# A two-layer hybrid trunk on one core: an ordered block for the first layer, a moved residual step, a rearranged last head and another form of the final norm

## The chip, the cores and the metric

The kernel runs on one core of one Trainium2 chip. The metric is the device time of one execution in microseconds (us). The engines have their own instruction queues and run beside each other: PE (TensorE, matmuls; PEld is its weight load), DVE (VectorE), ACT (ScalarE), POOL (GpSimd) and SP (SyncE, which here only issues DMAs). An engine takes its instructions strictly in the order in which they stand in its queue; an instruction that waits for a semaphore holds up all that stand behind it.

## The reference: what is computed

128 context tokens and 512 latent tokens (640 together, five tiles of 128) of width 1024 go through two layers. Layer 0 is gated grouped-query attention, 16 heads of 64 on 4 key/value heads; layer 1 is a bidirectional gated linear recurrence with 8 heads of 128.

```
for i in range(DEPTH):                                   # DEPTH = 2
    sh, sc, g = split(silu(cond) @ ada_w[i] + ada_b[i])  # adaLN, for c and for c_ctx
    h = x * (1 + sc) + sh
    if i % 2 == 0: out = attention(h)   # q,k RMS norm, axial rotary, softmax, silu gate, w_out
    else:          out = rec_mix(h)     # two scans, RMS norm of o, silu gate, w_out
    x = layer_norm(ALPHA * x + g * out, ln_gain[i], ln_bias[i])
```

All is float32. The outputs are both token sets after layer 1, the new key/value cache and the new states.

## The kernel before

Each float32 operand of a projection is split into a high and a low part (ACT casts the high part, DVE or POOL subtracts it to get the low one), and each product takes three matmuls: high by high, low by high, high by low. Activations stand with features on the partitions and the 640 tokens along the row, so that most tiles are 128x640. Times below are us from the start of the span.

*Lead-in (0 to 72).* The adaLN weights of layer 0 come in eight chunks of 1 MB, one for each 128 features of the input. For each chunk PE forms the products (`adaps`, L264), DVE and PE turn them into shift and scale (`ada_row`, `ada_out`), the input is modulated and split, and PE adds this slice's share of keys and values (`acc`, `kv_mms`). SP issues the loads of these chunks and of the weights (`raw`, through a ring of buffers) in one queue. Then comes the first q projection (`pmm`).

*Gate and attention (72 to 362).* The silu gate's projections (`gps`, L335 to 337) run beside the norm and rotary of q, which ends in split tiles `qs` that PE transposes (`qps`, L587) and ACT casts to `X`. For each of the four key/value heads come 16 score tiles of 128 queries by 640 keys (64 in all): PE forms `sc` (L730, L731), DVE takes the row maximum (L824), ACT the exponent with its sum (L827), DVE the reciprocal `rc` (L831), POOL multiplies `p` by it (L832), PE transposes `p` (`pt`, L839), the transposes are copied to `pts` (L735), and PE multiplies with the values (`pot`, L757). The q projection of the next head group, adaLN chunks and the split of the output weights are side work: `weave(att, side, SIDE_B)` lets the side generators emit pieces between those of attention by planned costs.

*Out projection and norm of layer 0 (362 to 445).* `out_mms` (L1002 to 1006) and the class `Norm`; its result goes to DRAM (`x1d`) and, transposed, to the input of layer 1.

*Recurrent heads (445 to 840).* Each of the 8 heads has its five projections (`rps`, `vgps`) on PE, and the scan `gla_gen` of the head before stands between them: seven levels in which PE forms 32 to 128 wide blocks (`lv`), DVE multiplies the decays into A (L1276, L1281) and halves their tables. Behind the scan come the states (`kp`, `sp`), the output (`op`), its RMS norm (`rsqrt`, a DVE and a POOL instruction), two DVE products into `on`, the transposes `oT` and the split `ghi`, `glo`. The class `Residual` (L1359 on) works on the side: `Residual.step()` takes up to two pieces of 128x256 of layer 0's result from DRAM, multiplies by the gain and adds the bias on POOL (L1379, L1380), stores them to `x1a`, and issues the next two loads, all on POOL's queue. There are 20 pieces. It is called at scan level 4, behind the copies to `At`, and behind each head's `rsqrt`.

*Last head and final norm (789 to 876).* The last head has no next projection beside it. `tail_gen` fills PE with parts of the output projection of layer 1 over the heads that are done (`out_part(tt, ks)`: token tile `tt`, heads `ks`, six matmuls for each head) and with four gate spreads (`spread`, L307 and L308: four transposes each, and a copy to `gate`). When the last head's `glo` is there, the five token tiles get their last head's share, and `Norm(1, tt, ...)` runs for each: `y` = `outp` times gate (L1026), plus the residual (L1027), `bn_stats` and `bn_aggr` (L1028, L1033), `rsqrt`, then (y − mean) times gain (L1042) and times rstd plus bias (L1043), each in two halves of 512 columns, and the output's DMA in two halves on SP and ACT. The fifth tile, the context's, runs last and in quarters.

What sets the order: the program is emitted by generators, and the framework's scheduler orders each engine's instructions from it by their dependences; those in `tc.keep_in_program_order` keep their place among each other. Before the change no part of the program is set apart from the rest.

Of the kernel before, what the change touches and what calls it, by code (L numbers as in the profile page):

```python
# [11 lines left out]
F32 = mybir.dt.float32  # L12
# [120 lines left out]
def hybrid_step(ctx: ExitStack, tc: tile.TileContext, a: dict, o: dict):  # L133
# [30 lines left out]
            self.st.close()  # L164


    small = const.tile([P, 66], F32, name="small")
    nc.scalar.dma_start(small, a["small"])
    sel = small[:, 16:18]
# [18 lines left out]
    def rsqrt(out, in_, scale, eps):  # L188
        n = in_.shape[-1]
        t = tiny.tile([P, NKV * TT], F32, tag="rs", name="rs_t")  # L190
        nc.vector.tensor_scalar(t[:, :n], in_, scale, eps, ALU.mult, ALU.add)  # L191
        nc.gpsimd.tensor_tensor(out, t[:, :n], mhalf[:, :n], ALU.pow)
# [105 lines left out]
        nc.vector.tensor_tensor(gcol, src, bias, ALU.add)  # L298
        return None if layer else lambda: spread(layer, c4, gcol)

    def spread(layer, c4, gcol):

        ps = bank1("gateps")
        for s in range(2):
            for j in range(2):
                col = bass.AP(gcol.tensor, gcol.offset + 2 * j + s, [list(gcol.ap[0]), [0, P]])
                nc.tensor.matmul(ps[:, (2 * s + j) * P:(2 * s + j + 1) * P], col, ident, start=True, stop=True)  # L307
        nc.vector.tensor_copy(gate[layer][:, :, c4 * CW:(c4 + 1) * CW], ps[:].rearrange("p (a b) -> p a b", a=2))  # L308

    def ada_gen(chunks):  # L310
        todo, last = None, None
# [676 lines left out]
    rings[:] = [wr]  # L988


    ph = Phase(4, 0)
    h1p = rpool("h1p", 1)
    h1lo = h1p.tile([P, KT, NT], F32R, tag="h1lo", name="h1lo")
# [14 lines left out]
    class Norm:  # L1008
        def __init__(self, layer, tt, ps=None, parts=2):
            self.layer, self.tt, self.w = layer, tt, D // parts  # L1010
            if layer == 0:
                ps = bank2("outp")
            self.ps = ps and [ps[:, nh, :] for nh in range(2)]
            if layer == 0:
                self.x = lnp.tile([P, D], F32, tag="x", name="x", bufs=2)
                nc.scalar.dma_start(self.x, xd[tt])
            else:
                self.x = resid.pop(tt)
            self.y = lnp.tile([P, D], F32, tag="y", name="y", bufs=2)
            self.st = tiny.tile([P, parts, 6], F32, tag=f"st{parts}", name="st")  # L1020

        def part(self, n, ps):
            s = slice(n * self.w, (n + 1) * self.w)
            y = self.y[:, s]
            g = gate[self.layer][:, 1 if self.tt == TS else 0, s]
            nc.vector.tensor_tensor(y, ps, g, ALU.mult)  # L1026
            nc.vector.scalar_tensor_tensor(y, self.x[:, s], ALPHA, y, ALU.mult, ALU.add)  # L1027
            nc.vector.bn_stats(self.st[:, n, :], y)  # L1028

        def finish(self):  # L1030
            x, y = self.x, self.y
            mv = tiny.tile([P, 2], F32, tag="mv", name="mv")
            nc.vector.bn_aggr(mv, self.st[:].rearrange("p a b -> p (a b)"))  # L1033
            rt = tiny.tile([P, 8], F32, tag="rstd", name="rstdl")
            rstd = rt[:, 0:1]
            rsqrt(rstd, mv[:, 1:2], 1.0, LN_EPS)
            for nh in range(2):
                s = slice(nh * 512, (nh + 1) * 512)
                if self.layer == 0:
                    nc.vector.tensor_scalar(y[:, s], y[:, s], mv[:, 0:1], rstd, ALU.subtract, ALU.mult)  # L1040
                else:
                    nc.vector.scalar_tensor_tensor(x[:, s], y[:, s], mv[:, 0:1], lng[:, s], ALU.subtract, ALU.mult)  # L1042
                    nc.vector.scalar_tensor_tensor(x[:, s], x[:, s], rstd, lnb[:, s], ALU.mult, ALU.add)  # L1043
                    (nc.sync, nc.scalar)[nh].dma_start(yd[self.tt][:, s], x[:, s])
            if self.layer == 0:
                nc.sync.dma_start(x1d[self.tt], y)

    drain(split_gs(range(6, 8)))
    h1hi = gsp.tile([P, KT, NT], F32R, tag="gs", name="h1hi")
# [178 lines left out]
    def gla_gen(h, H, last=False):  # L1228
# [30 lines left out]
        for lev in range(7):  # L1259
            nb = NT // (2 * w)  # L1260
            pt = wide(bank2("lv"))
            for c in range(TT):
                if lev < 5:
                    for b in range(4):
                        t0 = c * P + 32 * b
                        queue(nc.tensor.matmul(pt[32 * b:32 * b + 32, 32 * c:32 * c + 32], kc[:, t0:t0 + 32],  # L1266
                                               view(A, QB + t0, [[2 * w, 16 // w], [QF - QB + w, 2], [1, w]]),
                                               start=True, stop=True), c + b == 0)
                else:
                    for b in range(P // w):  # L1270
                        ko, qo = (KB, QB) if b % 2 else (KF, QF)
                        s0, t0 = c * P + w * b, c * P + w * (b ^ 1)
                        queue(nc.tensor.matmul(pt[w * b:w * b + w, w * c:w * c + w], A[:, ko + s0:ko + s0 + w],
                                               A[:, qo + t0:qo + t0 + w], start=True, stop=True), c + b == 0)
            kv = view(A, KF, [[KB - KF + w, 2], [2 * w, nb], [1, w]])
            nc.vector.tensor_tensor(kv, kv, view(cur, 1, [[2 * nb - 1, 2], [2, nb], [0, w]]), ALU.mult)  # L1276
            if lev < 4:
                kc = kcopy(2 * w)
            qv = view(A, QB, [[QF - QB + w, 2], [2 * w, nb], [1, w]])
            nc.vector.tensor_tensor(view(nxt, 0, [[1, 2 * nb]]), view(cur, 0, [[2, 2 * nb]]), view(cur, 1, [[2, 2 * nb]]), ALU.mult)  # L1280
            nc.vector.tensor_tensor(qv, qv, view(cur, 2 * nb + 1, [[-2 * nb - 1, 2], [2, nb], [0, w]]), ALU.mult)  # L1281
            if lev == 0:
                nc.scalar.copy(near, pt[:, :32 * TT])
            elif lev < 5:
                merge(lev, pt)
            if lev == 4:
                pt = wide(bank2("dg"))
                for c in range(TT):
                    for b in range(4):
                        t = slice(c * P + b * 32, c * P + (b + 1) * 32)  # L1290
                        nc.tensor.matmul(pt[32 * b:32 * b + 32, 32 * c:32 * c + 32], H["kd"][:, t], H["q"][:, t], start=True, stop=True)
                merge(0, pt)
                for b in range(4):
                    r = slice(32 * b, 32 * b + 32)
                    nc.gpsimd.tensor_copy(blocks(At[r, :], P)[:, :, r], blocks(near[r, :], 32))  # L1295
                residual.step()
            elif lev > 4:
                for b in range(P // w):
                    r, o_ = slice(w * b, w * b + w), slice(w * (b ^ 1), w * (b ^ 1) + w)
                    nc.scalar.copy(blocks(At[r, :], P)[:, :, o_], blocks(pt[r, :w * TT], w))  # L1300
            cur, nxt = nxt, cur
            w *= 2
            yield D_LEV
# [35 lines left out]
            nc.scalar.activation(on[:, cc], opw[:, cc], AF.Square, accum_out=ss[:, c:c + 1])  # L1339
        rstd = tiny.tile([P, 8], F32, tag="rstd", name="rstdo")  # L1340
        rsqrt(rstd[:, :TT], ss[:, :TT], 1.0 / P, NORM_EPS)
        residual.step()
        nc.vector.tensor_tensor(on[:].rearrange("p (a b) -> p a b", a=TT), opw[:, :NT].rearrange("p (a b) -> p a b", a=TT),
                                view(rstd, 0, [[1, TT], [0, P]]), ALU.mult)
# [68 lines left out]
    def out_part(tt, ks):  # L1413
        if tt not in outs:
            outs[tt] = bank2("outp")
        for k in ks:
            for nh in range(2):
                out_mms(outs[tt][:, nh, :], tt, nh, ghi, glo, [k], queued=(k, nh) == (ks[0], 0))

    for h in range(RH):  # L1420
        H = {} if h else H
        for n, dt in enumerate(proj_gen(h, H, False) if h else first):
            lane.advance(dt)
            if h == RH - 1 and n in (12, 14, 20, 21):
                wo_split((12, 14, 20, 21).index(n))
        if h == RH - 1:
            out_part(0, (0, 1))
        lane.add(gla_gen(h, H, h == RH - 1))
    while residual.todo or residual.live:
        residual.step()  # L1430
# [4 lines left out]

    def tail_gen():
        yield
        out_part(1, (0, 1))
        lane.finish(1)
        wo_split(4)  # L1440
        yield
        splits = iter((5, 6, 7))
        for tt, ks in ((0, (2, 3)), (1, (2, 3)), (0, (4, 5)), (1, (4, 5)), (0, (6,)), (1, (6,))):
            out_part(tt, ks)
            for n in splits:
                wo_split(n)
                break
            yield
        gate[1] = g2.tile([P, 2, D], F32, tag="A", name="gate1")
        for i in range(4):  # L1450
            spread(1, i, gcol1[:, i])
            if i % 2:
                yield
        out_part(2, (0, 1, 2))
        yield
        out_part(2, (3, 4, 5, 6))
        yield

    resid = {}
# [115 lines left out]
```

## Time and profile before

| | |
|---|---|
| median of 3 runs | 878.02 us (876.84 to 880.31) |
| profiled execution | 877.56 us |
| its span | 875.8 us, granted TensorE clock 0.992 |
| lead-in and first q projection (0 to 72) | 58.00 + 14.00 us, PE busy 46.49 + 14.00 |
| gate stage (72 to 125) | 53.00 us, PE busy 50.10 |
| out projection, norm 0 (362 to 445) | 83.00 us, PE busy 82.06 |
| seven heads (445 to 789) | 344.00 us, PE busy 340.80 |

The other stages stand with the prediction. A row of the timeline reads: start, duration of one, engine, line, operation, tile written and tiles read with their shapes, how many in a run, and in brackets the idle time of the engine before it and what ended that. A row of the waits reads: the waiting engine and line, what it waited for, total us, times, longest. PE's matmuls overlap: a fill matmul of 0.39 us starts 0.23 us behind the one before.

### The profile page before, as it was taken

To read this page: it belongs to the slowest core of one execution; us is meant where nothing else is said; L and a number is where in the kernel's file an instruction comes from. 1 tells how busy PE (TensorE), PEld (TensorE's weight loads), DVE (VectorE), ACT (ScalarE), POOL (GpSimd) and SP (SyncE) were. 2 spreads that over 40 slices of the span, in tenths; PEclk is the share of its full clock that TensorE was granted. 3 is DMA by queue.
4 is the path that set the end of the run, shared out by engine and by line. 5 is a ranking of instruction groups with operands and counts; after the bars stand their busy time and mean duration, and the time that the engine had idled before them with its cause. 6 is when DMAs were issued, how large, how long until landed. Compare 5 with 4: busy or idle time off the path is not lost. (4 is left out here: it accounts for less than half of the span.)

```text
span 875.8 us, 19258 instructions
## 1 busy us (share of the span) xinstructions
PE 828.6 (95%) x8124; PEld 736.7 (84%) x8124; DVE 533.2 (61%) x966; ACT 369.9 (42%) x732; POOL 205.5 (23%) x247
## 2 busy tenths in 40 slices
PE   6898999989999899899999999999999999999895
PEld 3588999878877666678999999999999999997785
DVE  3457335565746655586637486666667575848468
ACT  2232436544745765612434453444444434444200
POOL 0132002422424643610000132233232212111111
PEclk9999999999999999999999999999999999999998
DMA  9931112212212037171232313222322323212113
GB/s 358 407 113 55 61 61 73 98 49 98 97 49 98 1 124 261 56 280 60 72 97 65 91 55 120 61 98 79 101 83 68 81 90 109 89 47 74 55 52 117
DMA packets 30182, 89.86 MB, mean 103 GB/s; under 512 B 4400, under 2 KB 9008, under 8 KB 29072
## 3 DMA queue, kind: packets, MB, share of 16 engines
q1 hardware_dynamic: 19728, 72.03, 23.2%
q0 software_dynamic: 3168, 9.31, 4.0%
q10 hardware_dynamic: 7200, 7.29, 2.6%
q8 instruction: 64, 1.05, 0.5%
q14 instruction: 22, 0.18, 0.1%
HBM read 79.44 MB, written 9.18 MB: 101 GB/s over the span
## 5 line engine op out<-in xcount | busy, mean ns | idle before, releaser
L1128 PE MATMUL rps<-h1hi,rhi 128*128 128x320 f32 x368 | 117.0, 318 | 0.0
L1129 PE MATMUL rps<-h1lo,rhi 128*128 128x320 f32 x368 | 113.5, 308 | 0.0
L1130 PE MATMUL rps<-h1hi,rlo 128*128 128x320 f32 x368 | 113.4, 308 | 0.0
L832 POOL TENSOR_SCALAR p<-p,rc 128x640 f32<-128x640 f32 x64 | 54.1, 847 | 95.2 <-DVE rc L831 84.0
L224 DVE TENSOR_TENSOR rlo<-raw,rhi 128x1024 fp32r<-128x1024 f32 x32 | 46.1, 1444 | 42.7 <-ACT rhi L223 42.7
L1128 PEld LDWEIGHTS rps<-h1hi,rhi 128*128 128x128 f32 x368 | 69.2, 188 | 1.3
L1130 PEld LDWEIGHTS rps<-h1hi,rlo 128*128 128x128 f32 x368 | 69.1, 188 | 0.2 <-DVE rlo L224 0.2
L1129 PEld LDWEIGHTS rps<-h1lo,rhi 128*128 128x128 f32 x368 | 69.0, 188 | 0.0
L824 DVE TENSOR_REDUCE nm<-sc 128x1 f32<-128x640 f32 x64 | 52.3, 820 | 25.0 <-PE sc L731 24.5
L827 ACT ACTIVATE p<-sc,nm 128x640 f32<-128x640 f32 x64 | 51.1, 799 | 25.7 <-DVE nm L824 18.6
L223 ACT CAST rhi<-raw 128x1024 fp32r<-128x1024 f32 x32 | 33.5, 1050 | 60.4 <-PE rps L1129 56.2
L839 PE MATMUL pt<-ident,p 128*128 128x128 f32 x320 | 50.7, 278 | 5.3 <-POOL p L832 3.1
L1239 ACT COPY kc<-A 128x640 f32<-128x640 f32 x40 | 32.5, 812 | 51.0 <-PE lv L1266 31.8
L1118 PE MATMUL vgps<-rhi,h1hi 128*128 128x256 f32 x180 | 51.1, 284 | 0.0
L1120 PE MATMUL vgps<-rhi,h1lo 128*128 128x256 f32 x180 | 50.7, 282 | 0.0
L1119 PE MATMUL vgps<-rlo,h1hi 128*128 128x256 f32 x180 | 50.4, 280 | 0.0
L735 ACT COPY pts<-pt 128x512 f32<-128x512 f32 x64 | 36.2, 589 | 31.6 <-PE pt L839 31.3
L1295 POOL COPY At<-near 32x160 f32<-32x160 f32 x32 | 10.0, 313 | 165.6 <-DVE near L1256 164.6
L839 PEld LDWEIGHTS pt<-ident,p 128*128 128x128 f32 x320 | 37.3, 142 | 13.5 <-POOL p L832 4.8
L730 PE MATMUL sc<-kk,X 128*128 128x320 f32 x128 | 43.5, 347 | 2.4 <-ACT p L827 2.2
L335 PE MATMUL gps<-hhi,whi 128*128 128x320 f32 x128 | 40.8, 319 | 2.4 <-ACT X L589 2.4
L1118 PE MATMUL vgps<-wspare,h1hi 128*128 128x256 f32 x140 | 41.6, 297 | 0.0
(265 smaller groups left out, 2403.2 us busy)
## 6 DMA issues: line engine op xcount, KB each, us to landing
raw<-in_rec_w_in SPq DMA_DIRECT2D x40, 512.0 KB, 4.3
raw<-in_ada_w SPq DMA_DIRECT2D x32, 512.0 KB, 3.9
raw<-in_ada_w SPq DMA_DIRECT2D x8, 1024.0 KB, 11.2
raw<-in_attn_w_in SPq DMA_DIRECT2D x16, 512.0 KB, 5.0
raw<-in_attn_w_out SPq DMA_DIRECT2D x8, 512.0 KB, 5.4
raw<-in_rec_w_out SPq DMA_DIRECT2D x8, 512.0 KB, 4.2
h<-in_xT SPq DMA_DIRECT2D x8, 320.0 KB, 10.0
x1d<-y SPq DMA_DIRECT2D x5, 512.0 KB, 2.8
```

Source lines behind the costliest of these rows:

```text
L224: pin((lo_eng or nc.gpsimd).tensor_tensor(lo, raw, hi.bitcast(F32), ALU.subtract))
L730: nc.tensor.matmul(out, X[:, h, t0:t0 + P], kk[:, c, k0:k1], start=True, stop=False)
L824: nc.vector.tensor_reduce(nm[:, 0:1], sc[:, :, :320], AX.XY, ALU.max, negate=True)
L827: nc.scalar.activation(halves(p[:]), sc[:, :, :320], AF.Exp, bias=nm[:, 0:1], accum_out=su[:, 0:1])
L832: nc.gpsimd.tensor_scalar(p, p, rs[:, 0:1], 1.0, ALU.mult, ALU.mult)
L839: nc.tensor.transpose(pt[:, i * 256 + q * P:i * 256 + (q + 1) * P], ps[q][:, (k0 + i) * P:(k0 + i + 1) * P], ident)
L1118: nc.tensor.matmul(out, h1hi[:, k, t], hi, start=(k == 0), stop=False)
L1119: nc.tensor.matmul(out, h1hi[:, k, t], lo, start=False, stop=False)
L1120: nc.tensor.matmul(out, h1lo[:, k, t], hi, start=False, stop=(k == KT - 1))
L1128: nc.tensor.matmul(ps[:, j, :320], hi[:, k, :], h1hi[:, k, t], start=(k == 0), stop=False)
L1129: nc.tensor.matmul(ps[:, j, :320], hi[:, k, :], h1lo[:, k, t], start=False, stop=False)
L1130: nc.tensor.matmul(ps[:, j, :320], lo[:, k, :], h1hi[:, k, t], start=False, stop=(k == KT - 1))
```

## The change

Four edits.

1. Everything from the first loads to the end of attention is put into a block of its own, `tc.block(name="lead", schedule_with_timeline_sim=True)`. Within it the scheduler orders by a simulated time line. At its end each engine branches (L993 of the changed kernel) to what follows; there is no barrier there.
2. `residual.step()` is taken from scan level 4 and called twice behind each head's `rsqrt`.
3. `tail_gen` is rearranged: `out_part(1, (0,))` comes ahead of the last head's scan, the spreads go one at a time between the scan's levels with their copies on ACT (`nc.scalar.copy`), and more of the fill stands ahead of `op` and between `op` and `oT`.
4. For the four latent tiles the norm of layer 1 is formed another way (`finish_two_pass`): ACT copies `y` with a running sum, multiplies the sum by −1/D, and squares y − mean with a running sum; DVE makes two products over all 1024 columns; one DMA on SP writes the tile.

```diff
+    blk = tc.block(name="lead", schedule_with_timeline_sim=True)
+    blk.__enter__()
     small = const.tile([P, 66], F32, name="small")
...
-    def spread(layer, c4, gcol):
+    def spread(layer, c4, gcol, eng=None):
...
-        nc.vector.tensor_copy(gate[layer][:, :, c4 * CW:(c4 + 1) * CW], ps[:].rearrange("p (a b) -> p a b", a=2))
+        (eng or nc.vector.tensor_copy)(gate[layer][:, :, c4 * CW:(c4 + 1) * CW], ps[:].rearrange("p (a b) -> p a b", a=2))
...
+    blk.__exit__(None, None, None)
     ph = Phase(4, 0)
...
+            self.two_pass = layer == 1 and tt < TS
...
-            nc.vector.bn_stats(self.st[:, n, :], y)
+            if not self.two_pass:
+                nc.vector.bn_stats(self.st[:, n, :], y)
...
+        def finish_two_pass(self, rstd):
+            x, y = self.x, self.y
+            junk = lnp.tile([P, D], F32, tag="sq", name="sq")
+            sums = tiny.tile([P, 4], F32, tag="mv2", name="mv2")
+            nc.scalar.activation(junk, y, AF.Copy, accum_out=sums[:, 0:1])
+            nc.scalar.mul(sums[:, 1:2], sums[:, 0:1], -1.0 / D)
+            nc.scalar.activation(junk, y, AF.Square, bias=sums[:, 1:2], accum_out=sums[:, 2:3])
+            nc.vector.scalar_tensor_tensor(x, y, sums[:, 1:2], lng, ALU.add, ALU.mult)
+            rsqrt(rstd, sums[:, 2:3], 1.0 / D, LN_EPS)
+            nc.vector.scalar_tensor_tensor(x, x, rstd, lnb, ALU.mult, ALU.add)
+            nc.sync.dma_start(yd[self.tt], x)
...
                     nc.gpsimd.tensor_copy(blocks(At[r, :], P)[:, :, r], blocks(near[r, :], 32))
-                residual.step()
...
         residual.step()
+        residual.step()
...
         if h == RH - 1:
             out_part(0, (0, 1))
+            out_part(1, (0,))
         lane.add(gla_gen(h, H, h == RH - 1))
...
-        out_part(1, (0, 1))
+        out_part(1, (1,))
         lane.finish(1)
+        out_part(0, (2,))
         wo_split(4)
         yield
-        splits = iter((5, 6, 7))
-        for tt, ks in ((0, (2, 3)), (1, (2, 3)), (0, (4, 5)), (1, (4, 5)), (0, (6,)), (1, (6,))):
-            out_part(tt, ks)
-            for n in splits:
-                wo_split(n)
-                break
+        out_part(0, (3,))
+        out_part(1, (2,))
+        wo_split(5)
+        yield
+        gate[1] = g2.tile([P, 2, D], F32, tag="A", name="gate1")
+        for i, (tt, k) in enumerate(((1, 3), (0, 4), (0, 5), (1, 4))):
+            out_part(tt, (k,))
+            spread(1, i, gcol1[:, i], nc.scalar.copy)
+            if i < 2:
+                wo_split(6 + i)
             yield
-        gate[1] = g2.tile([P, 2, D], F32, tag="A", name="gate1")
-        for i in range(4):
-            spread(1, i, gcol1[:, i])
-            if i % 2:
-                yield
-        out_part(2, (0, 1, 2))
+        out_part(1, (5,))
         yield
-        out_part(2, (3, 4, 5, 6))
+        out_part(0, (6,))
+        out_part(1, (6,))
+        yield
+        out_part(2, (0, 1))
+        yield
+        out_part(2, (2, 3, 4, 5))
+        yield
+        out_part(2, (6,))
         yield
```

Where the scheduler puts the rows now is seen best at three places. Each row has its place in the engine's queue, the line (the changed kernel's lines are higher by 2 to 19), the operation, the tile written and those read, the shape and how many in a run.

The first is PE at the end of attention, the last score tiles of the last head group; `X_2730` and `X_2731` are the same q tile. Before:

```order
1444 L731 MATMUL sc<-klo,X_2730 128x320
1445 L839 MATMUL pt<-ident,p 128x128 x6
1446 L730 MATMUL sc<-kk,X_2730 128x320
1447 L731 MATMUL sc<-klo,X_2730 128x320
1448 L730 MATMUL sc<-kk,X_2730 128x320
1449 L731 MATMUL sc<-klo,X_2730 128x320
1450 L839 MATMUL pt<-ident,p 128x128 x3
1451 L730 MATMUL sc<-kk,X_2730 128x320
```

And now:

```order
1443 L733 MATMUL sc<-klo,X_2731 128x320
1444 L841 MATMUL pt<-ident,p 128x128 x10
1445 L732 MATMUL sc<-kk,X_2731 128x320
1446 L733 MATMUL sc<-klo,X_2731 128x320
1447 L732 MATMUL sc<-kk,X_2731 128x320
1448 L733 MATMUL sc<-klo,X_2731 128x320
1449 L759 MATMUL pot<-pts,vv 64x256 x10
1450 L841 MATMUL pt<-ident,p 128x128 x16
```

Two pairs of `sc` rows are one score tile. Before, the transposes come in threes and sixes between the score tiles; now they stand in runs of ten and more, and a product with the values stands between the last score tile and the transposes behind it.

The second is SP in the lead-in: the loads of the input (`h`), of the adaLN chunks (`ada_w`, raw_170 to raw_279 before, raw_171 to raw_280 now, 1 MB each), of the key/value weights and of the q and gate weights (`attn_w_in`, 512 KB each). Before:

```order
15 L200 DMA h_106<-in_xT 128x640
16 L208 DMA raw_198<-in_ada_w 128x2048
17 L200 DMA h_106<-in_xT 128x640
18 L200 DMA ck<-in_cache_k 128x256
19 L208 DMA raw_236<-in_ada_w 128x2048
20 L211 DMA raw<-in_attn_kv 128x1024
21 L200 DMA h_106<-in_xT 128x640
22 L208 DMA raw_279<-in_ada_w 128x2048
23 L200 DMA h_106<-in_xT 128x640
24 L211 DMA raw<-in_attn_w_in 128x1024 x12
```

And now:

```order
16 L202 DMA ck<-in_cache_k 128x256
17 L213 DMA raw<-in_attn_kv 128x1024
18 L202 DMA h_107<-in_xT 128x640 x2
19 L213 DMA raw<-in_attn_w_in 128x1024 x5
20 L210 DMA raw_199<-in_ada_w 128x2048
21 L213 DMA raw<-in_attn_w_in 128x1024
22 L213 DMA raw<-in_attn_kv 128x1024
23 L210 DMA raw_237<-in_ada_w 128x2048
24 L210 DMA raw_280<-in_ada_w 128x2048
25 L213 DMA raw<-in_attn_w_in 128x1024 x6
```

Five loads of 512 KB have moved ahead of the last three chunks, and a sixth stands among them.

The third is DVE in the final norm, from the first tile on; `x_9353` and `x_9355` before, `x_9361` and `x_9363` now, are the residuals of the first two token tiles, `mv` the statistics (now ACT's sums). Before:

```order
864 L1026 TENSOR_TENSOR y<-outp,gate_9672 128x512 x2
865 L1027 SCALAR_TENSOR_TENSOR y<-x_9353,y 128x512 x2
866 L1028 BN_STATS st<-y 128x6 x2
867 L1026 TENSOR_TENSOR y<-outp,gate_9672 128x512
868 L1033 BN_AGGR mv<-st 128x2
869 L1026 TENSOR_TENSOR y<-outp,gate_9672 128x512
870 L191 TENSOR_SCALAR rs_t<-mv 128x1
871 L1042 SCALAR_TENSOR_TENSOR x_9353<-y,mv,ln_9799 128x512 x2
872 L1043 SCALAR_TENSOR_TENSOR x_9353<-x_9353,rstdl,ln_9799 128x512 x2
```

And now:

```order
862 L1030 TENSOR_TENSOR y<-outp,gate_9494 128x512 x2
863 L1031 SCALAR_TENSOR_TENSOR y<-x_9361,y 128x512 x2
864 L1030 TENSOR_TENSOR y<-outp,gate_9494 128x512 x2
865 L1031 SCALAR_TENSOR_TENSOR y<-x_9363,y 128x512
866 L1062 SCALAR_TENSOR_TENSOR x_9361<-y,mv_9817,ln_9800 128x1024
867 L193 TENSOR_SCALAR rs_t<-mv_9817 128x1
868 L1031 SCALAR_TENSOR_TENSOR y<-x_9363,y 128x512
869 L1064 SCALAR_TENSOR_TENSOR x_9361<-x_9361,rstdl,ln_9800 128x1024
870 L1030 TENSOR_TENSOR y<-outp,gate_9494 128x512
```

The statistics' rows are gone, the first product now stands ahead of the `rs_t` that starts the `rsqrt` instead of behind it, and between `rs_t` and the second product there is one row of 512 columns of the next tile.

More of the change, by code (lines that the diff above doesn't have):

```diff
@@ L1027, in part @@
             nc.vector.scalar_tensor_tensor(y, self.x[:, s], ALPHA, y, ALU.mult, ALU.add)
-            nc.vector.bn_stats(self.st[:, n, :], y)
+            if not self.two_pass:
+                nc.vector.bn_stats(self.st[:, n, :], y)
         def finish(self):
             x, y = self.x, self.y
+            rt = tiny.tile([P, 8], F32, tag="rstd", name="rstdl")
+            rstd = rt[:, 0:1]
+            if self.two_pass:
+                return self.finish_two_pass(rstd)
             mv = tiny.tile([P, 2], F32, tag="mv", name="mv")
             nc.vector.bn_aggr(mv, self.st[:].rearrange("p a b -> p (a b)"))
-            rt = tiny.tile([P, 8], F32, tag="rstd", name="rstdl")
-            rstd = rt[:, 0:1]
             rsqrt(rstd, mv[:, 1:2], 1.0, LN_EPS)
```

## The prediction

> **What bounds the kernel now.** I read the page's busy line first, then the busy time by stage, then TensorE's waits stage by stage, and at the end the chain that ended last.
>
> ```profile
> PE 828.6 (95%) x8124; PEld 736.7 (84%) x8124; DVE 533.2 (61%) x966; ACT 369.9 (42%) x732; POOL 205.5 (23%) x247
> ...
> 125.00:362.00 237.00, 222.22 (x1832) 180.95 (x1831) 133.88 (x303) 132.51 (x287) 86.44 (x85) 0.99 0.26 89
> ...
> 789.00:840.00 51.00, 47.77 (x530) 39.04 (x529) 30.20 (x51) 16.54 (x34) 4.19 (x9) 1.00 0.17 56
> 840.00:876.00 36.00, 25.11 (x155) 22.33 (x154) 32.42 (x66) 0.00 (x0) 5.92 (x7) 0.91 0.30 102
> ```
>
> The columns of the stages are length, then busy time of PE, PEld, DVE, ACT and POOL. PE sets the pace everywhere but at the end: attention (125 to 362 us) leaves it idle for 237.00 − 222.22 = 14.8 us, the stage of the last head (789 to 840) for 51.00 − 47.77 = 3.2. Behind 840 us the longest column is DVE's, 32.42 of 36, and ACT does nothing there: the final norms are DVE's. So this change can save PE's waits (it takes no matmul away), and DVE's work at the end, and no more than these.
>
> ```profile
> PE acc L474 <- ACT hhi L457: 4.6, 6, 1.9
> ...
> PE pt L839 <- POOL p L832: 2.7, 4, 1.1
> PE sc L730 <- ACT p L827: 1.8, 6, 0.5
> PE qps L587 <- DVE rc L831: 1.1, 1, 1.1
> PE pot L757 <- DVE pts L735: 1.0, 2, 0.5
> ...
> PE lv L1273 <- DVE A L1281: 3.2, 4, 0.8
> ```
>
> These are PE's waits (total us, times, longest) of three windows: the lead-in (0 to 60), most of attention (200 to 362), and the layer of the recurrent heads (400 to 790), where one kind of wait is nearly all there is. Each is touched by one of the four edits, so I go edit by edit. All terms are against the profiled execution, 877.56 us (span 875.8 and 1.76 around it), which stands 0.46 below the median of 878.02. I count as no change what lies within 0.5% of it, 4.4 us: about what a measurement of this kernel can tell.
>
> **Edit 1, the ordered block.** It alters no work, only the rows' order on each engine, and adds one branch on each at its end. In the lead-in the matmuls of the adaLN chunks now stand behind whole kv products instead of within them; the 4.6 us of waits for the split input shrink a little, and adding the durations of PE's rows in the new order gives an end of the first q projection 0.7 us earlier, of which I take 0.5. Behind it stands the costliest single wait of the stage:
>
> ```profile
> 82.89 1.11 PE L587 MATMUL qps<-identr,qs 128*128 128x128 f32 x8 [0.40 <-DVE qs L580]
> 86.92 0.42 PE L335 MATMUL gps<-hhi,whi 128*128 128x320 f32 x1 [2.40 <-ACT X L589]
> ```
>
> The new order puts a fourth run of 24 gate matmuls ahead of the first eight `qps` transposes, and the gate matmul right behind them no longer carries the wait for ACT. Of 0.40 + 2.40 = 2.8 us I take 2.0, since ACT has a queue of its own there. **Lead-in and gate stage: −2.5**, bounds −4 (with 1.2 more of the 4.6) and +4. The upper bound is for the loads: five `attn_w_in` pieces now stand ahead of three adaLN chunks on SP.
>
> In attention every score tile goes PE `sc`, DVE maximum, ACT exponent, POOL `p` times `rc`, back to PE `pt`:
>
> ```profile
> L832 POOL TENSOR_SCALAR p<-p,rc 128x640 f32<-128x640 f32 x64 | 54.1, 847 | 95.2 <-DVE rc L831 84.0
> ...
> L824 DVE TENSOR_REDUCE nm<-sc 128x1 f32<-128x640 f32 x64 | 52.3, 820 | 25.0 <-PE sc L731 24.5
> L827 ACT ACTIVATE p<-sc,nm 128x640 f32<-128x640 f32 x64 | 51.1, 799 | 25.7 <-DVE nm L824 18.6
> ```
>
> The three means are 0.85 + 0.82 + 0.80 = 2.5 us; with the read of ACT's sum, the reciprocal and the handovers I put the chain at some 3.4. I summed the durations of PE's rows between a tile's last `sc` and its first `pt` in both orders. Before, the least is 2.1 us and six places lie under 3.4; in the new order the least is 5.5. So the 2.7 us of `pt` waits should go. For `sc` two tiles apart, which needs the exponent of the earlier tile, 12 places are too tight before and 10 after: 0.2 of the 1.8. From `pt` to `pot`, 6 before and 3 after: 0.4 of the 1.0. Three first `qps` of a group, though, come closer behind their projection (2.6, 4.0 and 1.6 us of PE work where there were 3.4, 7.1 and 2.3). I count those as still covered. **Attention: −3.3.** Bounds: −9, three fifths of the 14.8 idle; and +4.6, the cover that the three `qps` lose (0.8 + 3.1 + 0.7) turned wholly into waits.
>
> The branch at the block's end has no row in this trace. The nearest are those behind the launch's own branch, and PE's wait where the new one will stand:
>
> ```profile
> 0.85 0.27 DVE L172 MEMSET sil<- 128x256 f32 x1 [0.85 <-PEq L1561]
> ...
> 361.52 0.50 PE L1002 MATMUL outp<-wohi,hhi 128*128 128x512 f32 x1 [0.53 <-DVE gs L762]
> ```
>
> Each engine branches by itself, with no barrier. Launch and branch together cost 0.85 at most, and PE waits 0.53 there anyway. **+0.4**, bounds 0 and +0.9. Queued behind it are the two splits of gate block 6 on ACT and POOL, which PE first needs some 18 matmuls into the output projection.
>
> **Edit 2, the residual step.** POOL multiplies and adds a residual tile while DVE does the last scan levels:
>
> ```profile
> 669.09 0.81 DVE L1281 TENSOR_TENSOR A<-A,T 128x640 f32<-128x640 f32 x1
> ...
> 674.34 1.74 DVE L1281 TENSOR_TENSOR A<-A,Tb 128x640 f32<-128x640 f32 x1
> ...
> 674.64 0.74 POOL L1379 TENSOR_TENSOR rx<-rx,ln_g 128x256 f32<-128x256 f32 x1
> 675.47 1.20 POOL L1380 TENSOR_TENSOR rx<-rx,ln_b 128x256 f32<-128x256 f32 x1
> ...
> 676.23 0.80 PE L1273 MATMUL lv<-A 128*64 128x64 f32 x20 [0.80 <-DVE A L1281]
> ...
> 695.49 1.32 DVE L1345 TENSOR_TENSOR on<-on,g 128x640 f32<-128x640 f32 x1
> ```
>
> The same DVE operation takes 1.74 us beside POOL's two and 0.81 without, and PE stands 0.80 for it: in four heads, 3.2 us in all. With the step away from there DVE is back at 0.81, 0.93 earlier than now, which covers the 0.80. Behind the rsqrt one step stands already; it stretches `on<-on,g` to 1.32 and PE waits for nothing in these heads. Two steps there overlap `on` and the next weight's split. All of a step's instructions go along, the two operations, its store and the next loads on POOL's queue; the four residual loads that the tail needs come after head 6's steps at about 788 us, 50 us before use. **−3.2**, bounds −3.5 and 0. [...]
>
> **Edit 3, the last head's fill.** Four things move: one output-projection piece goes ahead of the scan, the gate spreads go one per level, their four copies (0.69 us each) leave DVE for ACT, and 12 matmuls come ahead of `op` and 6 more between `op` and `oT`, all 18 taken from behind `oT`.
>
> ```profile
> 823.02 1.16 PE L307 MATMUL gateps<-ident,gcol 128*128 128x128 f32 x8 [1.38 <-DVE gate L308]
> 824.01 0.39 PE L1331 MATMUL op<-v,At 128*128 128x128 f32 x2
> ...
> 832.10 0.74 PE L1350 MATMUL oT<-ident,on 128*128 128x128 f32 x5 [0.90 <-DVE on L1345]
> ...
> 833.71 0.88 DVE L1352 SCALAR_TENSOR_TENSOR glo<-oT,ngain,ghi 128x640 fp32r<-128x640 f32 x1 [1.75 <-ACT ghi L1351]
> ...
> 834.75 0.39 PE L1002 MATMUL outp<-w,ghi 128*128 128x512 f32 x1
> 834.98 0.39 PE L1005 MATMUL outp<-w,ghi 128*128 128x512 f32 x1
> ...
> 839.80 1.29 DVE L1026 TENSOR_TENSOR y<-outp,gate 128x512 f32<-128x512 f32 x2 [5.21 <-PE outp L1006]
> ```
>
> `op`: a fill matmul starts every 0.23 us (834.75 to 834.98), so 12 more are +2.8, less the 1.38 of the gate wait and some 0.2 of small ones: +1.2 (bounds 0 and +2.8). From `op` to the first norm: before, 839.80 − 824.01 = 15.8. After: `op` 2.8, 24 fill matmuls 5.6 (the DVE, POOL and ACT chain to `on` needs 5.1, so the 0.90 goes), `oT` 0.55, ghi and glo 1.9, six matmuls of the last head 1.4, start 0.2 = 12.4, or 3.4 less. **−2.2**, bounds −4 and 0; what is late next is glo, for which 6 matmuls (1.4) no longer fill 1.9 us.
>
> **Edit 4, the norm of the four latent tiles.**
>
> ```profile
> 90.64 1.22 DVE L224 TENSOR_TENSOR wlo<-raw,whi 128x1024 fp32r<-128x1024 f32 x1 [3.86 <-ACT whi L223]
> ...
> 842.21 1.28 DVE L1028 BATCH_NORM_STATS2 st<-y 128x6 f32<-128x512 f32 x2
> ...
> 844.72 1.41 DVE L1042 SCALAR_TENSOR_TENSOR x<-y,mv,ln 128x512 f32<-128x512 f32 x2
> ...
> 844.88 0.99 POOL L192 TENSOR_TENSOR rstdl<-rs_t,mhalf 128x1 f32<-128x1 f32 x1 [14.65 <-DVE rs_t L191]
> ...
> 816.73 1.01 ACT L1309 COPY kt<-kp 128x1024 f32<-128x1024 f32 x1 [1.62 <-PE kp L1307]
> ...
> 871.08 1.41 DVE L1043 SCALAR_TENSOR_TENSOR x<-x,rstdl,ln 128x512 f32<-128x512 f32 x2
> ```
>
> An operation holds DVE about 0.08 less than its row says, from start to start. So per tile DVE loses the statistics (1.20) and a tenth for their aggregate, and two pairs of 1.32 become two of about 1.21 over 1024 columns (no row shows this form; the nearest is the 128x1024 split at 1.22): 1.2 + 0.12 + 0.22 = 1.54 less, four times 6.2. ACT gets 1.01 twice and three small ones of 0.2 per tile, far under the 5 us of a tile. But DVE's first product waits now for ACT's sum, and its second for POOL's 0.99 with nothing but one half tile between. Laying the new DVE order out with these durations leaves waits of 0.58, 0.54, 0.78 and 0.75 before the second products: 2.65 given back, −3.5 net. Before, the norms last from 839.80 to 871.08 + 1.41 = 872.49, 32.7 us. PE ends some 25 us behind the first norm operation (25.11 us of work behind 840), and some four of DVE's must follow it, so more than 32.7 − 29 = 3.7 can't be saved. I take **−3.0**, bounds 0 (all waits twice as long) and −4.
>
> **Sum:** −2.5 − 3.3 + 0.4 − 3.2 − 2.2 − 3.0 = −13.8; 877.56 − 13.8 = **863.8 us**.
>
> **Rivals.**
> *The block gives nothing.* Waits there only change places; the row for is that `sc` keeps 10 tight places of 12, the row against is the 2.40 at 86.92. Then −2.5 and −3.3 fall away: 869.6.
> *The waits come back behind the other edits.* The POOL steps hold `on` in seven heads by up to 0.7 as they held A (5 us, more than the 3.2; the rows show 0.5 per head and no PE wait), and the norms wait for POOL and ACT as long as DVE saves. With edits 2 and 4 at 0 and edit 3 at −1: 877.56 − 5.4 − 1 = 871.2. [...] With the block at nothing too: 877.0.
> *Slower: the new attention order starves PE at `pt`.* POOL multiplies `p` 64 times; where it came late PE stood up to 1.1 us. If the new order packs the tiles so that POOL or ACT falls behind, each stand costs about that. The other terms sum to −10.5, so from 14 of 64 stands on (15 us) the kernel is slower; a third of them, 21, gives 23 us and 890. Against it: no place under 5.5 us.
>
> **Numbers.** Forecast 0.50; block at nothing 0.22; waits back 0.10; both 0.10; starved 0.08. That the change is without effect is in "both". The range runs from 854 (the better bounds of attention and lead-in) to 875.5; it leaves out the slower rival, half of "both" and little below. Under 873.2 lie the forecast and most of the next two: faster 0.78; same 0.14; slower 0.08.
>
> **What would show it.** Right: no PE wait near 0.80 for DVE's A in the heads, and that operation at 0.81; `pt` waits for POOL gone; no 2.4 at the first `gps` behind `qps`; PE idle between 125 and 362 us near 11; first norm operation 11 us or so earlier by the clock; some 29 to 30 us from there to the last DVE operation, where it was 32.7. Wrong: PE waiting for an adaLN chunk between 35 and 50 us, `qps` waiting for `qs`, `oT` for `on`, or DVE standing over 1 us for rstd in each norm.

## The result and the profile after

The changed kernel takes 870.46 us (median of 5 runs, 868.67 to 871.34) where the kernel before took 878.02: 7.6 us less, a ratio of 0.9908 with a 95% interval of 0.9888 to 0.9927. Its profiled execution took 868.67 us, the least of its five, with a span of 866.9 against 875.8, so the traces have 8.9 us to account for. The forecast was 863.8. Of the kernels below, one execution of e2 (1598.55 us) and one of e5 (1144.59 us) were far slower than all the others, and their medians are given without them.

The page's busy line first (busy time, share of the span, instructions):

```profile
PE 827.0 (95%) x8124; PEld 739.7 (85%) x8124; DVE 528.8 (61%) x942; ACT 382.5 (44%) x756; POOL 205.9 (24%) x247
```

The matmuls are the same 8124. DVE has 24 instructions less and ACT 24 more. Where the time went is read best from a few events that both programs have: the last matmul of the first q projection, the first matmul of the out projection, its first wait, the first transposes of layer 1's input, and the first and last DVE operation of the final norms. These are rows of the timeline of the changed kernel:

```profile
74.93 0.28 PE L346 MATMUL pmm<-whi,hlo 128*128 128x256 f32 x1
...
356.25 0.50 PE L1005 MATMUL outp<-wohi,hhi 128*128 128x512 f32 x1 [0.53 <-DVE gs L764]
371.86 0.47 PE L1005 MATMUL outp<-wohi,hhi 128*128 128x512 f32 x1 [3.77 <-DVE y L1030]
384.70 1.04 PE L1082 MATMUL h1t<-ident,y 128*128 128x128 f32 x8
...
787.92 1.32 DVE L1364 TENSOR_TENSOR on<-on,g 128x640 f32<-128x640 f32 x1
834.29 1.29 DVE L1030 TENSOR_TENSOR y<-outp,gate 128x512 f32<-128x512 f32 x2 [1.33 <-PE outp L1009]
862.46 1.41 DVE L1050 SCALAR_TENSOR_TENSOR x<-x,rstdl,ln 128x512 f32<-128x512 f32 x2
```

And the same events before, as far as they were not shown yet:

```profile
71.65 0.28 PE L344 MATMUL pmm<-whi,hlo 128*128 128x256 f32 x1
384.37 1.03 PE L1063 MATMUL h1t<-ident,y 128*128 128x128 f32 x8
789.98 0.82 DVE L1345 TENSOR_TENSOR on<-on,g 128x640 f32<-128x640 f32 x1
```

Each difference of two events, after less before, is one piece of the 8.9 us:

| piece | predicted | measured |
|---|---|---|
| lead-in, to the end of the first q projection (74.93 against 71.65) | −0.5 | +3.3 |
| gate stage and attention, to the first out-projection matmul | −2.0 − 3.3 = −5.3 | −8.6 |
| from there to the first `h1t` (28.45 us against 22.85) | +0.4 | +5.6 |
| recurrent heads, to `on` of head 6 | −3.2 | −2.4 |
| last head, to the first norm operation | −2.2 | −3.5 |
| norms, first to last DVE operation (29.6 against 32.7) | −3.0 | −3.1 |
| behind the last DVE operation | 0 | −0.3 |
| sum | −13.8 | −9.0 (of single roundings; the spans differ by 8.9) |

Edits 2 to 4 gave 9.0 of a forecast 8.4. The block gave +0.3 of a forecast −5.4: it was 5.3 us ahead at the first out-projection matmul, and had lost all of it 28 us later. Three more views say how.

The first is PE's waits of the changed kernel (total us, times, longest), 0 to 60 and then 125 to 362:

```profile
PE acc L476 <- ACT hhi L459: 4.5, 3, 1.8
PE adaps L289 <- DVE row L280: 1.6, 3, 0.5
PE adaps L266 <- DMA raw<-in_ada_w: 1.5, 1, 1.5
...
PE sc L732 <- ACT p L829: 2.8, 8, 0.7
PE qps L589 <- DVE qs L582: 2.7, 1, 2.7
PE adaps L289 <- DVE gcol L300: 2.6, 1, 2.6
PE pt L841 <- ACT pts L737: 1.5, 4, 0.5
```

In the lead-in the wait for the split input, six waits before and three now, is as long as it was, and 2.6 us of others came to it. In attention no wait for POOL's `p` is left, as forecast, but two single waits of 2.7 and 2.6 us stand there. The one for `gcol` is new; the one for `qs` stood at an earlier head group before. These are its rows, before and after:

```profile
192.06 0.52 PE L587 MATMUL qps<-identr,qs 128*128 128x128 f32 x4 [2.77 <-DVE qs L580]
...
298.33 0.52 PE L589 MATMUL qps<-identr,qs 128*128 128x128 f32 x4 [2.72 <-DVE qs L582]
```

The second is DVE at the block's end. Before:

```profile
363.87 4.43 DVE L224 TENSOR_TENSOR wolo<-raw,wohi 128x1024 fp32r<-128x1024 f32 x2 [2.41 <-ACT wohi L223]
368.22 0.68 DVE L1026 TENSOR_TENSOR y<-outp,gate 128x512 f32<-128x512 f32 x1
368.82 2.82 DVE L224 TENSOR_TENSOR wolo<-raw,wohi 128x1024 fp32r<-128x1024 f32 x1
371.57 3.42 DVE L224 TENSOR_TENSOR rlo<-raw,rhi 128x1024 fp32r<-128x1024 f32 x1
```

And after:

```profile
358.61 7.79 DVE L226 TENSOR_TENSOR wolo<-raw,wohi 128x1024 fp32r<-128x1024 f32 x3 [2.41 <-ACT wohi L225]
366.33 3.39 DVE L226 TENSOR_TENSOR rlo<-raw,rhi 128x1024 fp32r<-128x1024 f32 x1
...
369.81 1.21 DVE L226 TENSOR_TENSOR rlo<-raw,rhi 128x1024 fp32r<-128x1024 f32 x1
...
371.03 0.68 DVE L1030 TENSOR_TENSOR y<-outp,gate 128x512 f32<-128x512 f32 x1
```

The first norm product `y`, for which PE's third accumulation waits, stood between the splits of the output weights; now it stands behind all of these and behind two splits (`rlo`) for the layer after. A split takes 2.2 to 3.4 us here, while POOL makes splits too (its rows stand from 357.02 to 368.63 in the changed kernel), instead of the 1.21 of the last one, behind them.

The third is the granted clock. These are windows of 2 us of the changed kernel (length, busy time of PE, PEld, DVE, ACT, POOL with their counts, then PE's granted clock, the DMA share and GB/s), from the lead-in, behind a wait of 1.85 us, and from behind the wait of 3.77 us:

```profile
36.00:38.00 2.00, 1.18 (x5) 1.00 (x6) 0.84 (x2) 0.72 (x1) 0.00 (x0) 1.00 1.01 406
38.00:40.00 2.00, 2.00 (x7) 1.50 (x6) 0.00 (x0) 0.00 (x0) 0.00 (x0) 0.50 1.06 432
40.00:42.00 2.00, 2.00 (x7) 1.36 (x5) 0.00 (x0) 1.44 (x2) 0.00 (x0) 0.65 1.00 414
...
372.00:374.00 2.00, 2.00 (x7) 1.52 (x8) 1.93 (x4) 0.00 (x0) 0.00 (x0) 0.63 1.00 389
374.00:376.00 2.00, 2.00 (x6) 1.61 (x5) 1.18 (x2) 0.00 (x0) 0.00 (x0) 0.52 0.82 283
376.00:378.00 2.00, 2.00 (x10) 1.59 (x10) 0.00 (x0) 0.00 (x0) 0.00 (x0) 1.00 0.67 262
```

Behind both waits the granted clock falls to half for some 3.4 us and then comes back: 2 x (0.37 + 0.48) = 1.7 us of matmul time lost behind the second, on top of the wait. With the 3.77 this makes 5.5 of the 5.6 us.

### The profile page after: what moved, and what is told of

Its sections match the earlier page's. It is cut to its first block, busy times and chain, and to the rows that moved or that the text cites. A ratio compares the mean times of both kernels' runs of the same rounds, so it can differ in the third digit from the quotient of the medians.

```text
span 866.9 us, 19259 instructions
## 1 busy us (share of the span) xinstructions
PE 827.0 (95%) x8124; PEld 739.7 (85%) x8124; DVE 528.8 (61%) x942; ACT 382.5 (44%) x756; POOL 205.9 (24%) x247
## 4 chain that ended last, share of the span: by engine, by line
PE 83%; DVE 5%; ACT 4%; issue 4%; DMA 3%; POOL 1%; SPq 0%; ACTq 0%; DVEq 0%; POOLq 0%
PE rps L1147 7%; PE rps L1149 7%; PE rps L1148 6%; PE vgps L1137 5%; PE vgps L1139 4%; PE vgps L1138 4%; PE pot L759 4%; PE pt L841 4%; PE outp L1005 3%; PE outp L1009 2%; PE outp L1008 2%; PE adaps L266 2%; PE gps L337 2%; PE lv L1285 2%; PE gps L338 2%
## 5 line engine op out<-in xcount | busy, mean ns | idle before, releaser
L226 DVE TENSOR_TENSOR rlo<-raw,rhi 128x1024 fp32r<-128x1024 f32 x32 | 44.1, 1380 | 46.0 <-ACT rhi L225 46.0
L194 POOL TENSOR_TENSOR rstdo<-rs_t,mhalf 128x5 f32<-128x5 f32 x8 | 9.5, 1192 | 162.3 <-DVE rs_t L193 162.3
```

The costliest lines, as they stand in the source:

```text
L226: pin((lo_eng or nc.gpsimd).tensor_tensor(lo, raw, hi.bitcast(F32), ALU.subtract))
```

## The experiments

Ten kernels were run; each median is compared with runs of the kernel before on the same chip (877.0 to 877.5 there). Theory A is the table above: the block nets nothing because of where its order puts a few rows; edits 2 to 4 carry the gain.

**e1, the changed kernel without the block.**

```diff
-    blk = tc.block(name="lead", schedule_with_timeline_sim=True)
-    blk.__enter__()
...
-    blk.__exit__(None, None, None)
```

> The changed kernel without its ordered block; edits 2 to 4 stay. Theory A (read from the two traces): the block nets nothing, since the 5.3 us that it had won by the first out-projection matmul are gone 28 us later; then this runs like the changed kernel, 869 to 872 us, with PE's waits of 2.4 and 2.8 us of the kernel before back in the gate stage and in attention, and no wait of 3.8 us for DVE's first y behind the block. Rival B (the sum of the prediction): the block is worth 5.4 us, and this runs at 875 to 876.

868.38 us, ratio 0.9899 (0.9886 to 0.9911), where the changed kernel has 0.9908 (0.9888 to 0.9927): the same without the block. Rival B, by which the block is worth 5.4 us, falls. The waits of 2.41 (gate stage) and 2.76 us (`qps`) are back in its trace, and there is none for `y`.

**e2, the kernel before with the block alone.** The same lines added.

> The kernel before with the ordered block alone. Theory A: no change, 877 to 879.5 us: lead-in 3 us longer, first out-projection matmul some 5 us earlier, the first h1t transposes at the same time as before (384 us). Rival B: 872 to 873.

879.37 us, ratio 1.0021 (1.0009 to 1.0034). By itself the block costs some 2 us: q projection to 74.25, first out-projection matmul at 357.48 with the wait of 3.80 behind it, first `h1t` at 385.89 against 384.37.

**e3, the residual steps alone.**

```diff
-                residual.step()
...
         residual.step()
+        residual.step()
```

> The kernel before with the residual steps alone moved behind rsqrt. Theory A: the four waits of 0.8 us for DVE's A go and nothing comes for them: 3.2 us less, 874 to 875.5. Rival: the overlap with POOL moves to the product on<-on,g and the next weight split and PE waits there: 877 to 879.

874.15 us, ratio 0.9965 (0.9953 to 0.9976): 2.9 us less. None of the four waits of 0.8 us for DVE's A is left in the trace (one of 0.7 us, for another product of A, stands at the start of the last head), so the rival, that the overlap costs as much behind the rsqrt, falls.

**e4, the first norm product ahead of the next layer's splits.**

```diff
-        norms[tt].part(nh, norms[tt].ps[nh])
+        with tc.high_priority() if (tt, nh) == (0, 0) else nullcontext():
+            norms[tt].part(nh, norms[tt].ps[nh])
```

> The changed kernel with the first layer's first norm product of the first tile given priority, so that DVE does it ahead of the two splits of the next layer's weights instead of behind them. Theory A: the wait of 3.8 us at the third tile of the out projection goes, and with it the 4 us at about half clock right behind it: 5 to 5.5 us less than the changed kernel, 864.5 to 866. Rival C: the low clock has another cause and stays: 3.4 us less, 866.5 to 868. Rival D: PE then waits for the weight splits that have become later: 869 to 872.

866.13 us, ratio 0.9872 (0.9858 to 0.9886). On DVE, `y` now stands right behind the three output splits and ahead of the first `rlo`:

```profile
362.65 7.76 DVE L226 TENSOR_TENSOR wolo<-raw,wohi 128x1024 fp32r<-128x1024 f32 x3 [2.41 <-ACT wohi L225]
370.34 0.68 DVE L1030 TENSOR_TENSOR y<-outp,gate 128x512 f32<-128x512 f32 x1
370.94 2.82 DVE L226 TENSOR_TENSOR rlo<-raw,rhi 128x1024 fp32r<-128x1024 f32 x1
```

The wait is gone and so is the low clock behind it: first out-projection matmul to first `h1t` took 383.49 − 360.29 = 23.2 us, as before the change (22.85). That is 5.2 us at the place, as theory A has it. The medians show less, 4.3 us against the changed kernel's run and 3.2 by the two ratios, so they alone don't tell theory A from C; in e4's profiled execution the clock fell twice in the lead-in, once at 186 us, and behind the wait for `gcol` for 6.8 us instead of 3.4, where the changed kernel's trace has one fall in the lead-in and the short one behind `gcol`. That is three falls of 1.7 us more, and its first out-projection matmul comes 4.0 us later (360.29 against 356.25).

**e5 and e6, edits 3 and 4 alone** on the kernel before: `tail_gen`, `spread` and the one `out_part` ahead of the scan for e5, the class `Norm` for e6.

> The kernel before with the last head's rearranged fill alone. Theory A: the first norm operation comes 3 to 3.5 us earlier against the end of head 6, and nothing behind it changes: 3.4 us less than before, 873.5 to 875. Rival: the fill matmuls put ahead of op delay op by as much as the others gain: 876.5 to 878.

> The kernel before with the final norm's other form alone. Theory A: the norms from the first DVE operation to the last take 29.6 us where they took 32.7: 3.1 us less, 873.8 to 875.5. Rival: half of this needs the rearranged fill, since PE hands over its last tile late: 875.5 to 877.

e5: 873.71 us, ratio 0.9964 (0.9950 to 0.9978). `on` of head 6 to the first norm operation 838.05 − 791.63 = 46.4 us, where it was 49.8: theory A. e6: 875.58 us, ratio 0.9976 (0.9967 to 0.9984), 1.9 us less, which lies just within the rival's interval. Its mechanism does not show: the norms took 29.8 us in the trace of e6, its fastest execution, so what they save (2.9) is there without the rearranged fill. Why the median shows only two thirds of it stays open.

**e7 to e9, the lead-in's order.** e7 is e4 with PE's matmuls of the lead-in held in the order of the program, e9 is e4 with SP's loads held so, e8 has both.

```diff
+    def lead_mm(*args, **kw):
+        ins = nc.tensor.matmul(*args, **kw)
+        return tc.keep_in_program_order(ins) if leading[0] else ins
...
+    def lead_dma(*args):
+        ins = nc.sync.dma_start(*args)
+        return tc.keep_in_program_order(ins) if leading[0] else ins
...
-                lead_mm(acc[tt], hhi[:, ft, t], hi, start=(ft == 0), stop=False)
```

The last line stands for all matmuls of `ada_part`, `ada_out` and `kv_mms` and for the loads of `pump`, which call these helpers instead of the engine.

> The kernel of e4_y_first, with PE's matmuls of the lead-in kept in the order in which the program has them (each adaLN chunk and its shift and scale within the kv product of the chunk before), SP's queue as the ordered block has it. Theory A: the lead-in's 3 us come from PE's order, which leaves the chain from adaLN product to split input uncovered (1.85 us, twice or three times) and lets the clock fall to half once or twice: first q projection ends at 72 us, 3 to 4.5 us less than e4, 861.5 to 863.5. Rival: they come from SP's order, the adaLN chunks behind five weight loads, and PE waits for the DMA between 33 and 45 us: 865 to 867.

862.82 us, ratio 0.9831 (0.9810 to 0.9853). The time lies within theory A's interval, but the trace shows the rival's mechanism: PE, in the program's order, stands for the sixth chunk, whose load SP issued behind five others. The first row is PE's wait, the next two are SP's in the same trace, and the last is the load of the sixth chunk in the kernel before, 11 us earlier.

```profile
38.55 1.94 PE L201 MATMUL adaps<-raw,sil 128*32 128x256 f32 x16 [4.68 <-DMA raw<-in_ada_w]
...
21.32 5.75 SPq L218 DMA_DIRECT2D raw<-in_attn_w_in  x5
27.98 0.33 SPq L215 DMA_DIRECT2D raw<-in_ada_w  x1
...
16.71 0.33 SPq L208 DMA_DIRECT2D raw<-in_ada_w  x1
```

> As e7_lead_pe_order, with SP's loads of the lead-in too in the order that the program has. Theory A: no further change against e7, within 0.7 us. Rival: if e7 stands at 865 or more, this one shows the 3 us, 862 to 863.5.

856.14 us, ratio 0.9759 (0.9745 to 0.9773): 6.7 us less than e7, and the first q projection ends at 67.5 us. Neither expectation had this; theory A's "within 0.7 us" is refuted.

> As e8_lead_pe_sp_order, but with SP's loads alone kept in the program's order and PE's matmuls of the lead-in as the ordered block has them. Theory A (from e7 and e8): the lead-in needs both orders, since with PE's order as the block has it each chain from adaLN product to split input of 1.85 us stands uncovered; three such waits and one or two falls of the clock stay: 3 to 6 us more than e8, 859 to 862. Rival: the late adaLN chunks alone made the lead-in long, also in PE's order of the block, and this runs like e8, 855.5 to 857.5.

856.85 us, ratio 0.9775 (0.9760 to 0.9790): the rival. SP's order alone does it. The waits of its lead-in (0 to 60):

```profile
PE adaps L201 <- ACT sil L177: 6.2, 1, 6.2
PE adaps L201 <- DVE row L289: 1.7, 3, 0.6
PE adaps L201 <- DMA raw<-in_ada_w: 1.4, 1, 1.4
```

There is no wait for `hhi` left, though no PE row was held: with SP's loads held, the scheduler puts PE's products in another order, in which the chain to the split input is covered. I take it from this that PE's order in the changed kernel, with its 1.85 us gaps, had been arranged around the late chunks. So of the two it was SP's order, with the five weight loads ahead of the sixth chunk. Held so, SP's loads come in the order that they have in the kernel before, and `y` stands ahead of the next layer's splits as it does there; so e9 against e1, 0.9775 against 0.9899, is what the block gives beside these two: some 11 us.

**e10, the block with these orders on the kernel before,** without edits 2 to 4.

> The kernel before with the ordered block and the three orders of e4, e7 and e8 (y first, PE's and SP's lead-in as in the program), without edits 2 to 4. Theory A: the block's gain and those of edits 2 to 4 add up: e8 stands 21.4 us below the kernel before, edits 2 to 4 alone (e1) 8.7, so this is 12 to 13 us below, 864 to 866. Rival: the first layer's gain is partly lost again in the recurrent heads when their waits are back: 868 to 870.

865.65 us, ratio 0.9864 (0.9851 to 0.9878): within theory A's interval, 11.4 us below the kernel before; the parts add up to within a microsecond or two (11.4 + 8.7 = 20.1, e8 against its runs of before 21.4). The block is worth some 11 us once `y` and SP's loads are put right, and −2 us (e2) without. e8 and e9 are the fastest kernels of this study, 2.4 and 2.25% below the kernel before.

## Why the prediction was right, and where it was wrong

The sign and the size of edits 2 to 4 were right, each by its own mechanism (together −9.0 of −8.4 forecast). The time came out 6.7 us above the forecast, though within the range: 4.9 us of that is in the traces, where the block gave 5.7 less than forecast and the other edits a little more, and the rest is that the profiled execution lies 1.8 us below its median.

That the block's error stayed so small is partly luck, since one of its terms came out 3.3 us better than forecast and two came out 3.8 and 5.2 worse. The time stands nearer to the first rival, the block at nothing (869.6), than to the forecast, but not by that rival's mechanism: the waits in attention did go, and what they gave was lost in the lead-in and behind the block. One sum of the prediction is wrong: the better bounds of attention and lead-in, 5.7 and 1.5 us better than the terms taken, give 856.6 us for the lower end of the range, not 854.

*The block's end, +0.4 forecast, +5.6 measured: the step that failed.* The prediction priced the branch and what ACT and POOL have behind it. The branch itself cost nothing: PE waits 0.53 for `gs` at that place in both traces. It did not ask what moved on DVE behind the branch, where the order shows `y` behind two more splits, and it did not lay `y` against the time when PE needs the accumulator again. Both were to be had: 48 matmuls at 0.23 us are 11.0 us from the first `outp`, while five splits at the 2.2 to 3.4 us that the rows of before show there take 11 us at least, from a start 2.4 us behind the first `outp` (363.87 against 361.52), and `y` comes only then (measured, its end is at 371.03 + 0.68 − 356.25 = 15.5 us). That e4 takes away the wait with this one row moved shows the cause.

*The lead-in, −0.5 forecast, +3.3 measured.* The sum of PE's rows in the new order was no measure here, since the order was made around loads that came later. The loads were named, with a bound of +4, "five `attn_w_in` pieces now stand ahead of three adaLN chunks on SP", and then taken as harmless. They were not: e9, which differs from e4 in SP's order alone, ends the q projection 8.6 us earlier (its last row starts at 66.86 against 75.47). What showed in the changed kernel was not the wait for a chunk that the prediction told to look for, but gaps of PE's order that came from it.

*Gate stage and attention, −5.3 forecast, −8.6 measured.* The mechanism held in part: no wait for POOL's `p` is left, and the 2.40 behind `qps` is down to 0.4, but the `sc` waits for ACT, taken as 0.2 us less, grew from 2.2 to 2.8 us. The wait of 2.77 us at 192 us went without having been forecast, since the prediction's view of attention began at 200 us; against it stand the new one for `gcol` and that for `qs` at 298 us, which the prediction had named as a sign of being wrong: of the three `qps` that come closer behind their projection, all taken as covered, one was not. Idle time between 125 and 362 us is 12.75, not the 11 foretold. Over the whole piece PE's idle time fell by only 4.3 us (17.7 to 13.4), less than the 5.3 forecast; the other 4.3 are busy time of PE (271.9 to 267.6), which the prediction took as fixed. One fall of the clock less accounts for 1.7 of these (below): the waits of 2.40 and 2.77 us each had one behind them, the wait for `gcol` has one. The remaining 2.6 us stay open.

*The residual step, −3.2 forecast, −2.4 here and −2.9 alone (e3).* The four waits went, and PE's idle time from the first `h1t` to `on` of head 6 fell by 3.1 us; PE's busy time there rose by 0.7, for a reason that the views don't show. The same operation on A takes, over the heads (operation, count, busy time, mean ns), before and after:

```profile
L1281 DVE TENSOR_TENSOR A<-A,Tb 128x640 f32<-128x640 f32 x21 | 20.9, 997 | 7.2 <-PE lv L1266 7.2
...
L1300 DVE TENSOR_TENSOR A<-A,Tb 128x640 f32<-128x640 f32 x21 | 18.3, 873 | 2.1 <-PE lv L1285 2.0
```

DVE's time on A did not fall as a whole: its four kinds of row there (L1276 and L1281 before, L1295 and L1300 now) took 84.3 us over the heads and take 85.1, for 98 rows each time. Behind `on`, the weight split takes 2.2 us where a second piece of POOL's runs beside it and 1.2 where none does, in three and two heads, before (2.18, 2.19, 2.19 and 1.21, 1.21) as now (2.19, 2.20, 2.20 and 1.22, 1.21). In the head shown here DVE's split starts first (695.34 against 695.69 for POOL's piece) and is lengthened all the same:

```profile
694.10 1.32 DVE L1364 TENSOR_TENSOR on<-on,g 128x640 f32<-128x640 f32 x1
695.34 2.20 DVE L226 TENSOR_TENSOR rlo<-raw,rhi 128x1024 fp32r<-128x1024 f32 x1
```

PE did not wait for such a split in any head, and `on<-on,g` has a median of 1.32 us in both traces, 0.5 above its least (0.82 and 0.83); the up to 0.7 that a rival put on it was an estimate that no run shows, and that rival did not come about.

*The last head, −2.2 forecast, −3.5 measured*, here and in e5 (46.4 us against 49.8). The mechanism held: from `op` to the first norm operation it took 12.2 us, where 12.4 were forecast. Mis-sized was `op`'s delay, +0.1 (34.2 us behind `on` against 34.0) and not the +1.2 taken.

*The norm, −3.0 forecast, −3.1 measured.* DVE's two long products and the waits for rstd, foretold as 0.58, 0.54, 0.78 and 0.75, in the first tiles:

```profile
840.89 1.28 DVE L1064 SCALAR_TENSOR_TENSOR x<-x,rstdl,ln 128x1024 f32<-128x1024 f32 x1 [0.45 <-POOL rstdl L194]
...
845.10 1.28 DVE L1064 SCALAR_TENSOR_TENSOR x<-x,rstdl,ln 128x1024 f32<-128x1024 f32 x1 [0.47 <-POOL rstdl L194]
...
852.06 1.28 DVE L1064 SCALAR_TENSOR_TENSOR x<-x,rstdl,ln 128x1024 f32<-128x1024 f32 x1 [0.22 <-POOL rstdl L194]
...
855.63 1.28 DVE L1064 SCALAR_TENSOR_TENSOR x<-x,rstdl,ln 128x1024 f32<-128x1024 f32 x1 [0.70 <-POOL rstdl L194]
```

## What to carry to other kernels

When a scheduler re-orders a stage, compare every engine's queue at its two ends first, the DMA queue and the first rows behind it: one DVE row behind the boundary and five loads in SP's queue turned some 11 us into −2. Ask of each consumer that frees a buffer when its producer needs it again, in rows, and not only what it costs. A wait of PE of 2.4 us or more was dearer here than it reads, since in three of four cases (22 of 28) the clock fell with it.

## What the runs showed of the hardware that was not expected

The fall of the clock. At the start of each trace the column of the granted clock reads 1.00 though PE's rows are nearly twice as long there (in the kernel before, 16 `adaps` take 1.94 us at 6.28 and 1.07 at 18.97), so the first 16 us are left aside. Behind them, in the twelve traces (before, after, e1 to e10), the granted clock fell to half in or behind 19 of the 25 waits of PE of 2.4 to 2.8 us, all three of 3.8 and 4.7 us and 3 of 5 of 1.8 to 2.0, and behind none of the 22 from 1.0 to 1.4. Three falls (e1 and e5 near 300 us, e4 at 186) stand behind no single wait of 1 us or more, but behind two or three shorter ones within 3 us (0.89 and 0.58; 0.70, 0.52 and 0.38); what brought them stays open. Here is the one at 86.92 us in the kernel before, which the prediction read as 2.4 us:

```profile
86.00:88.00 2.00, 1.08 (x7) 1.08 (x8) 0.69 (x1) 1.35 (x4) 0.00 (x0) 0.94 0.00 0
88.00:90.00 2.00, 2.00 (x9) 2.00 (x9) 0.00 (x0) 0.44 (x1) 0.00 (x0) 0.50 0.00 0
90.00:92.00 2.00, 2.00 (x12) 2.00 (x11) 1.22 (x1) 0.60 (x1) 0.00 (x0) 0.70 0.02 4
92.00:94.00 2.00, 2.00 (x16) 2.00 (x15) 0.80 (x1) 1.39 (x2) 0.00 (x0) 1.00 0.58 203
```

Such a fall costs 2 x (0.06 + 0.50 + 0.30) = 1.7 us. Of the 28 falls, 23 last 3.4 us like this one, and five (e4, e5, e7, e8, e10) last 6.8 us, twice as long. A wait of 2.7 us of `qps` for `qs` brings a fall in 6 of the 12 traces and none in the others; what decides between them was not shown. Such a wait thus cost 2.7 us in some traces and 2.7 + 1.7 = 4.4 in others, and this may be why kernels with such waits spread by several us from run to run. The runs on record fit this: the fastest run of e7, 860.37 us, has a mean granted clock of 0.992, the slowest, 866.36, one of 0.985. That idleness is the cause was not tried by itself, with PE kept busy in a wait; e4 shows only that the fall went with the wait. One more thing in the traces speaks for it: in all twelve the clock falls to half 2.0 to 5.1 us behind PE's last matmul, when PE has nothing left to do.
